# Where GpSimd scales and shifts the residual rows: in the up stages, in half rows through DRAM, not during the down projections

## The chip, the cores and the metric

One core of a Trainium2 chip (trn2) runs the whole program. The metric is the device time of one execution in microseconds (us); three timed executions and one profiled execution of the kernel before are shown.

## The reference

Two layers over 1024 rows of 1024 float32 numbers. Layer 0's mixer is a gated delta network, layer 1's is retention. Cut to what the change touches:

```python
e = silu(c @ cond_w + cond_b)
for i in range(2):
    sh1, sc1, g1, sh2, sc2, g2 = split(e @ ada_w[i] + ada_b[i], 6)
    y = mixers[i](x * (1 + sc1) + sh1)
    x = layer_norm(ALPHA * x + (1 + g1) * y, ln_g[i, 0], ln_b[i, 0])
    gate, up = split((x * (1 + sc2) + sh2) @ ffn_up[i], 2)      # 1024 -> 2 x 2816
    y = (silu(causal_dwconv(gate, ffn_conv_w[i]) + ffn_conv_b[i]) * up) @ ffn_down[i]
    x = layer_norm(ALPHA * x + (1 + g2) * y, ln_g[i, 1], ln_b[i, 1])
```

`layer_norm` standardizes a row, multiplies it by `ln_g` and adds `ln_b`. The kernel keeps the first norm's rows standardized only and folds `ln_g` and `ln_b` into the scale and shift of the feed-forward input. The residual term `ALPHA * x` of the second norm needs the rows with gain and shift applied, and that is the step that the change moves.

## The kernel before

`layer_tail(i, ...)` runs from a layer's mixer output to its end. It has three parts.

**The prologue and the up stage** are `strassen`. Its prologue multiplies the first items by plain blocks and meanwhile builds the combined right-hand blocks T1 to T4 (`build_T` with its closure `rest`, lines 395 to 437: VectorE subtractions and additions of SBUF tiles). Then come pairs of items, `fp` from 0 to 10: a gate item with `conv` behind it (line 1535: the causal convolution on VectorE) and an up item (line 1549: the product with the gate). When the fourth quarter of an up item is done, GpSimd forms the four sums S1 to S4 of the left-hand blocks (line 1556), and the SP queue stores them to the DRAM tile `ad` (line 1540). Weights come in through tiles `wr` (lines 102, 1210 and 1211), which the SP queue loads.

**The down projection** is `proj_gen`: seven products p of 11 steps j. Each step splits a left block (`ar` to `ab`) and a right block (`Bw`, `Br` to `bb`) into two parts: ScalarE rounds the tile, and VectorE subtracts (line 90). TensorE multiplies them on lines 278 to 280.

**The residual rows** of the first norm lie standardized in `x_mid` (DRAM, `xs[0]` and `xs[2]`), and `proj_gen` applies gain and shift on GpSimd. In the first products `gain_half` takes the second 512 rows in eight half rows of 128x512: a load into a `lane` tile by SP (line 1339), a multiplication and an addition (line 1341), and a store to `xg[i + 1]` by GpSimd's own DMA queue (line 1342). In product 2 `xload` loads the first 512 rows from `x_mid` as four whole rows and scales them in place, 16 operations on half rows (line 1349). Later `xload(1, t)` reads the second half back from `xg` without further work, and `finish` (lines 1354 to 1357) adds the residual.

**What sets the order.** No order is written out for most of the program. When it is built, a scheduler places each instruction on its engine's queue as soon as its operands and its buffers are free by the scheduler's own estimate of times; the place in the program text decides among those that are ready. A tag such as `auh` or `lane` is a set of buffers that are handed out in program order: 8 of 128x512 for `auh`, 4 of 128x1024 for `lane`. `after("w")` ties a DMA behind the last weight load of the program text. Each queue then runs strictly in order, and a DMA that waits for a semaphore holds what stands behind it on its queue.

Of the `auh` buffers a layer holds two with the row `rows[i, 2]` (gate of the mixer's output, read on lines 333 or 1354 to the end of the mixer projection), two with `rows[i, 5]`, and four with gain and shift (`gain_rows`, line 198). `trig` (line 1603) takes four for the cosines and sines of layer 1's retention; it stands behind the whole of layer 0 in the program.

`bg_gain` (lines 370 to 387) does the same scaling for the norm between the layers, on 16 half rows: load by SP (line 380), two GpSimd operations (381, 382), store by SP (383). It is not changed.

Of the kernel before, what the change touches and what calls it, by code (L numbers as in the profile page):

```python
# [33 lines left out]
def trunk_kernel(ctx: ExitStack, tc, A):  # L34
# [47 lines left out]
    def hs(half):  # L82
        return slice(half * HALF, (half + 1) * HALF)
# [281 lines left out]
    def gain_rows(n, key, tag="auh"):  # L365
        return [row_load(A[nm][n:n + 1, :], key, sp, tag) for nm in ("ln_g", "ln_b")]
# [895 lines left out]
            return raw  # L1262
        return ablk

    def proj_gen(nj, ablk, wsrc, slots, xsrc, G, final, ln_next, tag, ltags, dst, key, mm=pe.matmul, gate=None, gain=None):
        bal = {nm: BAL[ltags[4] + nm] for nm in ABLK + ("w11", "w21", "w22", "wT1", "wT2", "wT3", "wT4", "n", "h")}
        pa = [tl("aux", [P, 2, HALF], name="pa") for _ in range(4)]
        p1 = [pa[t // 2][:, t % 2] for t in range(4)]
# [61 lines left out]

        xts = [[], []]
        stats = [[], []]
        grows = gain_rows(gain[0], key) if gain else None

        def gain_half(n):
            hf, rs = n // 4, slice(HALF + n % 4 * P, HALF + (n % 4 + 1) * P)
            x = tl("lane", [P, HALF], name="xg")
            with after("w"):
                sp.dma_start(x, gain[1][rs, hs(hf)])
            for r, op in zip(grows, (ALU.mult, ALU.add)):  # L1340
                pool.tensor_tensor(x, x, r[hf], op)
            pool.dma_start(xsrc[rs, hs(hf)], x)

        def xload(half, t):
            xt = load_row(xsrc if half or not gain else gain[1], half, t)
            if half == 0 and gain:
                for r, op in zip(grows, (ALU.mult, ALU.add)):
                    for hf in range(2):
                        pool.tensor_tensor(xt[:, hs(hf)], xt[:, hs(hf)], r[hf], op)
            xts[half].append(xt)  # L1350
            stats[half].append(tl("st", [P, 2, 6]))

        def finish(half, t, nh, c):
# [74 lines left out]
        for p, (an, bn, fin) in enumerate(prods):  # L1428
            accs = acc4() if gate and p < 2 else [acc_next() for _ in range(4)]
            tail = []  # L1430
            depth = ltags[3] if p == 6 else 2
            for j in range(nj):
                if gate and p < 2:
                    yield gate(j)
                    yield from take("qkv", 2)
                    give("qkv", 2)
                a, w = ops(an, bn, j, not gate and p < (7 if final else 5))
                with after("a"):
                    for st in steps[p * nj + j + ahead:p * nj + j + ahead + 1]:
                        load_b(*st)  # L1440
                if gain and p < 2 and j % 2 == 0 and p * 4 + j // 2 < 8 and j < 8:
                    gain_half(p * 4 + j // 2)
                if gain and p == 2 and j % 2 == 0 and j < 8:
                    xload(0, j // 2)
                if p == 2 and j < 4 and gate:
                    xload(0, j)
                    finish(0, j, 0, c11[j])
                if j >= nj - depth:
                    tail.append((j, a, w))
                else:  # L1450
                    for t in range(4):
                        mma(accs[t], t, a, w, j == 0, False, mm if p < 2 else pe.matmul)
                        yield 0.0
                if p == 5 and j > 1:
                    for _ in range(-(-16 // (nj - 2))):
                        if hooks:
                            hooks.pop(0)()
                bg_step()
            if p == 5:
                while hooks:  # L1460
                    hooks.pop(0)()
            if p == 6:
                pin[0] = None
            for t in range(4):
                for j, a, w in tail:
                    mma(accs[t], t, a, w, j == 0, j == nj - 1, mm if p < 2 else pm if p == 6 else pe.matmul)
                fin(t, accs[t])
                yield 0.0
            if p == 1:
                yield "P2"  # L1470
            if p == 4:
                hooks = [] if final else ln_hooks(0, xts[0], tag, ln_next, outs, dst, key, bal["h"])
                hooks += [lambda t=t: xload(1, t) for t in range(4)]
# [12 lines left out]
    def layer_tail(i, mix, wout, xsrc, x_mid, x_out, ln_next, final):  # L1486
        sc2, sh2 = fold(i, 1, 2 * i)
        if i == 0:
            hT0 = []
            get = out_hl(mix)  # L1490
            G1 = rows[0, 2]
            xts = proj_ln(0, GH, get, wout, xsrc, G1, ("x", i))
            hooks = ln_hooks(0, xts, "hTa", lambda: (sc2, sh2), hT0, x_mid, ("mid", i), BAL["gh"])
            xts = proj_ln(1, GH, get, wout, xsrc, G1, ("x", i), hooks=hooks)
            hooks = ln_hooks(1, xts, "hTa", lambda: (sc2, sh2), [], x_mid, ("mid", i))
            for h in hooks[KT:]:
                h()
        else:
            mix.append((sc2, sh2))
            hT0, xts = proj_st(mix[0])  # L1500
        bg_ada(i, 5, "row")
        if i == 0:
            for j in (1, 0, 4, 3):
                bg_ada(1, j, "col")
        cw = vcol(f"ffn_conv{i}")
        cb = vcol(f"ffn_convb{i}")
        ad = dr.tile([NF // 2, 7, P, HALF], F32, tag=f"ad{i}", name=f"ad{i}")
        up = A["ffn_up"][i]

        def pair_items(fp):  # L1510
            g, o = [], []

            def gate_start():
                g.extend(tl("lane", [P, D], name="g") for _ in range(2))

                def gate(q, a, b):
                    dst = g[q // 2][:, hs(q % 2)]
                    if b is None:
                        act.activation(dst, a, AF.Copy)
                    else:  # L1520
                        dve.tensor_tensor(dst, a, b, ALU.add)
                return gate

            def conv():
                for q in range(4):
                    f, hf = 2 * fp + q // 2, q % 2
                    gv = g[q // 2]
                    w = cw[:, 3 * f:3 * f + 3]
                    t = tl("qkv", [P, HALF], name="o")
                    act.activation(t, gv[:, hs(hf)], AF.Copy, scale=w[:, 2:3])  # L1530
                    for j in (1, 2):
                        c0 = HALF if hf else j
                        c1 = HALF * (hf + 1)
                        tv = t[:, c0 - HALF * hf:]
                        dve.scalar_tensor_tensor(tv, gv[:, c0 - j:c1 - j], w[:, 2 - j:3 - j], tv, ALU.mult, ALU.add)  # L1535
                    act.activation(t, t, AF.Silu, bias=cb[:, f:f + 1])
                    o.append(t)

            def store(nm, q):
                sp.dma_start(ad[fp, ABLK.index(nm)], o[q])  # L1540

            def up_start():
                seen = []

                def gated(q, a, b):
                    c = a
                    if b is not None:
                        dve.tensor_tensor(c, a, b, ALU.add)
                    dve.tensor_tensor(o[q], o[q], c, ALU.mult)  # L1549
                    if q != 1:  # L1550
                        store({0: "11", 2: "12", 3: "22"}[q], q)
                    seen.append(q)
                    if len(seen) == 4:
                        for d, x, y, op, nm in ((1, 1, 3, ALU.add, "S1"), (0, 1, 0, ALU.subtract, "S2"),
                                                (2, 2, 0, ALU.subtract, "S4"), (3, 3, 0, ALU.subtract, "S3")):
                            pool.tensor_tensor(o[d], o[x], o[y], op)  # L1556
                            store(nm, d)
                return gated

            return [(up[4 * fp], up[4 * fp + 2], gate_start, conv), (up[4 * fp + 1], up[4 * fp + 3], up_start, None)]  # L1560

        strassen(hT0, xts, sc2, sh2, [it for fp in range(NF // 2) for it in pair_items(fp)])
        slots = {"c": "hTa", "x": "qkv"}
        gb2 = gain_rows(3, ("mid", i), "hTb") if final else None
        return proj_st(proj_gen(NF // 2, ablk_of(ad, "qkv"), A["ffn_down"][i], slots, xg[i + 1], rows[i, 5],
                       (gb2, x_out) if final else None, ln_next, "hTb", ("hTb", "hTa", 8, 6, "f") if final else ("qkv", "hTa", 8, 4, "0"), x_out, ("out", i), gain=(2 * i, x_mid)))

    g1 = two("auh", F32, "g1")
    for nh in range(2):
# [352 lines left out]
```

## Time and profile before

| what | value |
|---|---|
| median of 3 runs | 3033.51 us (3031.15 to 3038.18) |
| the profiled execution | 3032.61 us |
| its span, first to last instruction | 3030.8 us |
| mean granted TensorE clock | 0.971 |
| TensorE busy | 2840.2 us (94%) |
| VectorE busy | 2271.4 us (75%) |
| ScalarE busy | 1316.8 us (43%) |
| GpSimd busy | 672.8 us (22%) |

In the rows PE is TensorE, PEld its weight loads, DVE VectorE, ACT ScalarE, POOL GpSimd and SP the queue that issues most DMAs; a q behind an engine's name is its sequencer. L90 is line 90. Rows of the timeline give the start in us, the duration in us, the engine, line, operation, output and input, and the count of merged instructions. Rows of the stretches give for each engine the busy us and, in brackets, the count of instructions; then the granted clock, the DMA share and GB/s. By the trace, the prologue of layer 0 lies at about 770 to 860 us, its up stage reaches to about 1215, and its down projection to about 1440; in layer 1 the three begin at about 2343, 2440 and 2790.

### The profile page before, as it was taken

What the parts mean: (1) busy time and instruction counts of PE and PEld (TensorE: products, weight loads), DVE (VectorE), ACT (ScalarE), POOL (GpSimd) and SP (SyncE); (2) the same over time, 40 slices, a digit from 0 to 9 for tenths busy, and PEclk for the clock granted to TensorE, in tenths of its full rate; (3) what the DMA queues carried; (4) which work ended last, traced back from release to release, by engine and by line L of the source; (5) the groups of instructions that cost most, each with busy time, mean ns of one, the idle gap of its engine ahead of it and who ended that gap; (6) DMA issues with size and microseconds to landing.
All of it is one profiled execution on the core that took longest, in us unless ns stands there. A gap on an engine that the chain in (4) does not pass through costs nothing. (4 is left out here: it accounts for less than half of the span.)

```text
span 3030.8 us, 38796 instructions
## 1 busy us (share of the span) xinstructions
PE 2840.2 (94%) x13590; PEld 2312.4 (76%) x13590; DVE 2271.4 (75%) x3841; ACT 1316.8 (43%) x2408; POOL 672.8 (22%) x629
## 2 busy tenths in 40 slices
PE   8889998999999999998999999999999899999997
PEld 7768876887778788786777787767777678888785
DVE  5785786545888888998788645566688887778988
ACT  4655555434544445445432442222243544445442
POOL 0410311033021111730023303422200011113704
PEclk9999998999999999999999999999998999999998
DMA  7222221354344545854322444666663332336663
GB/s 271 89 70 74 98 82 62 116 170 138 106 153 151 158 158 182 309 193 141 126 105 98 166 160 144 200 184 186 202 217 132 98 136 104 105 105 227 232 188 108
DMA packets 243027, 450.22 MB, mean 149 GB/s; under 512 B 22928, under 2 KB 76432, under 8 KB 242832
## 3 DMA queue, kind: packets, MB, share of 16 engines
q1 hardware_dynamic: 211648, 400.02, 40.0%
q10 hardware_dynamic: 29760, 43.00, 3.9%
q0 software_dynamic: 1424, 4.72, 0.4%
q8 instruction: 107, 1.75, 0.2%
q14 instruction: 88, 0.72, 0.1%
HBM read 339.13 MB, written 108.53 MB: 148 GB/s over the span
## 5 line engine op out<-in xcount | busy, mean ns | idle before, releaser
L636 PE MATMUL acc<-hT,wh 128*128 128x512 f32 x960 | 302.8, 397 | 0.0
L1556 POOL TENSOR_TENSOR o<-o 128x512 f32<-128x512 f32 x88 | 121.1, 1386 | 725.4 <-DVE o L1549 622.9
L279 PE MATMUL acc<-bb,ab 128*128 128x512 f32 x504 | 205.5, 408 | 18.8 <-DVE bb L90 18.7
L1158 PE MATMUL acc<-T,wb 128*128 128x512 f32 x840 | 205.3, 393 | 8.7 <-DVE wb L90 8.6
L636 PEld LDWEIGHTS acc<-hT,wh 128*128 128x128 f32 x960 | 184.3, 192 | 34.5
L278 PE MATMUL acc<-bb,ab 128*128 128x512 f32 x504 | 192.2, 407 | 16.9 <-DVE ab L90 10.3
L636 PE MATMUL acc<-hT,wl 128*128 128x512 f32 x480 | 204.3, 426 | 0.3 <-ACT sg L1084 0.3
L89 ACT ACTIVATE ab<-ar 128x512 fp32r<-128x512 f32 x210 | 129.8, 624 | 168.6 <-PE acc L280 87.9
L280 PE MATMUL acc<-bb,ab 128*128 128x512 f32 x504 | 202.6, 403 | 0.0
L1158 PEld LDWEIGHTS acc<-T,wb 128*128 128x128 f32 x840 | 157.9, 189 | 46.1 <-DVE wb L90 12.4
L90 DVE TENSOR_TENSOR wb<-wr,wb 128x512 fp32r<-128x512 f32 x162 | 116.0, 718 | 92.8 <-ACT wb L89 89.5
L90 DVE TENSOR_TENSOR ab<-ar,ab 128x512 fp32r<-128x512 f32 x210 | 169.2, 812 | 15.1 <-ACT ab L89 14.7
L90 DVE TENSOR_TENSOR wl<-wr,wh 128x1024 fp32r<-128x1024 f32 x85 | 106.4, 1252 | 89.7 <-ACT wh L89 89.7
L90 DVE TENSOR_TENSOR wb<-mm,wb 128x512 fp32r<-128x512 f32 x216 | 145.1, 683 | 22.8 <-ACT wb L89 20.9
L89 ACT ACTIVATE wh<-wr 128x1024 fp32r<-128x1024 f32 x101 | 106.8, 1058 | 121.3 <-PE acc L636 56.1
L89 ACT ACTIVATE wb<-mm 128x512 fp32r<-128x512 f32 x216 | 122.8, 593 | 72.5 <-DVE mm L1204 72.4
L1215 ACT ACTIVATE pc<-acc 128x512 f32<-128x512 f32 x143 | 84.5, 593 | 154.0 <-PE acc L1158 95.2
L636 PE MATMUL acc<-wh,hT 128*128 128x512 f32 x384 | 138.0, 422 | 2.0 <-DVE vv L90 2.0
L89 ACT ACTIVATE wb<-wr 128x512 fp32r<-128x512 f32 x162 | 99.3, 627 | 92.2 <-DMA wr<-in_ffn_up 45.9
L1535 DVE SCALAR_TENSOR_TENSOR o<-g,vc,o 128x512 f32<-128x512 f32 (+2 forms) x176 | 138.2, 804 | 0.8 <-ACT o L1530 0.2
L457 DVE SCALAR_TENSOR_TENSOR qkv<-raw,vc,qkv 128x512 f32<-128x512 f32 x144 | 114.6, 800 | 30.4 <-ACT qkv L455 29.3
L279 PEld LDWEIGHTS acc<-bb,ab 128*128 128x128 f32 x504 | 98.9, 196 | 44.7 <-DVE bb L90 24.3
(634 smaller groups left out, 7792.0 us busy)
## 6 DMA issues: line engine op xcount, KB each, us to landing
wr<-in_ffn_up SPq DMA_DIRECT2D x96, 512.0 KB, 4.0
mvw<-in_ada_w SPq DMA_DIRECT2D x80, 512.0 KB, 4.3
ad<-o SPq DMA_DIRECT2D x154, 256.0 KB, 2.2
ar<-ad SPq DMA_DIRECT2D x154, 256.0 KB, 4.4
Br<-in_ffn_down SPq DMA_DIRECT2D x88, 256.0 KB, 4.1
wr<-in_ret_wv SPq DMA_DIRECT2D x32, 512.0 KB, 3.7
ar<-od SPq DMA_DIRECT2D x56, 256.0 KB, 5.3
xs<-xt ACTq DMA_DIRECT2D x24, 512.0 KB, 3.8
```

Source lines behind the costliest of these rows:

```text
L89: act.activation(dst_h, src, AF.Copy)
L90: eng.tensor_tensor(dst_l, src, dst_h, ALU.subtract)
L278: mm(acc, a[1][:, sl], w[0], start=first, stop=False)
L279: mm(acc, a[0][:, sl], w[1], start=False, stop=False)
L280: mm(acc, a[0][:, sl], w[0], start=False, stop=last)
L457: dve.scalar_tensor_tensor(oh, raw[:, 3 - j:515 - j], w[:, 3 - j:4 - j], oh, ALU.mult, ALU.add)
L636: pq(pe.matmul(out, lhsT, rhs, start=start, stop=stop), cost)
L1158: return pe.matmul(*a, skip_group_check=True, **kw)
L1215: act.activation(t, X, AF.Copy)
L1535: dve.scalar_tensor_tensor(tv, gv[:, c0 - j:c1 - j], w[:, 2 - j:3 - j], tv, ALU.mult, ALU.add)
L1556: pool.tensor_tensor(o[d], o[x], o[y], op)
```

## The change

The four rows of gain and shift are loaded ahead of the up stage. A function `scale_rows` takes one half row of 128x512 at each call: load from `x_mid` by SP into an `auh` tile, multiplication and addition on GpSimd, store to `xg[i + 1]` by SP. It is called behind each `conv` but the first pair's, and ahead of S1 to S4 of each up item; the first 16 of its 21 calls have a half row to do. `proj_gen` loses `gain_half` and the scaling in `xload`; product 2 now loads the first 512 rows from `xg`, as whole rows.

```diff
@@ proj_gen
-        grows = gain_rows(gain[0], key) if gain else None
-
-        def gain_half(n):
-            hf, rs = n // 4, slice(HALF + n % 4 * P, HALF + (n % 4 + 1) * P)
-            x = tl("lane", [P, HALF], name="xg")
-            with after("w"):
-                sp.dma_start(x, gain[1][rs, hs(hf)])
-            for r, op in zip(grows, (ALU.mult, ALU.add)):
-                pool.tensor_tensor(x, x, r[hf], op)
-            pool.dma_start(xsrc[rs, hs(hf)], x)
-
         def xload(half, t):
-            xt = load_row(xsrc if half or not gain else gain[1], half, t)
-            if half == 0 and gain:
-                for r, op in zip(grows, (ALU.mult, ALU.add)):
-                    for hf in range(2):
-                        pool.tensor_tensor(xt[:, hs(hf)], xt[:, hs(hf)], r[hf], op)
-            xts[half].append(xt)
+            xts[half].append(load_row(xsrc, half, t))
...
-                if gain and p < 2 and j % 2 == 0 and p * 4 + j // 2 < 8 and j < 8:
-                    gain_half(p * 4 + j // 2)
-                if gain and p == 2 and j % 2 == 0 and j < 8:
+                if not gate and p == 2 and j % 2 == 0 and j < 8:
                     xload(0, j // 2)
@@ layer_tail
+        grows = gain_rows(2 * i, ("mid", i))
+        scaled = [(hf, r) for hf in range(2) for r in range(8)]
+
+        def scale_rows():
+            if scaled:
+                hf, r = scaled.pop(0)
+                rs = slice(r * P, r * P + P)
+                x = tl("auh", [P, HALF], name="xg")
+                sp.dma_start(x, x_mid[rs, hs(hf)])
+                for w, op in zip(grows, (ALU.mult, ALU.add)):
+                    pool.tensor_tensor(x, x, w[hf], op)
+                sp.dma_start(xg[i + 1][rs, hs(hf)], x)
...
             def conv():
+                if fp:
+                    scale_rows()
                 for q in range(4):
...
                     if len(seen) == 4:
+                        scale_rows()
                         for d, x, y, op, nm in ((1, 1, 3, ALU.add, "S1"), (0, 1, 0, ALU.subtract, "S2"),
```

More of the change, by code (lines that the diff above doesn't have):

```diff
@@ L1263, in ablk_of, with proj_gen @@
         return ablk
-    def proj_gen(nj, ablk, wsrc, slots, xsrc, G, final, ln_next, tag, ltags, dst, key, mm=pe.matmul, gate=None, gain=None):
+    def proj_gen(nj, ablk, wsrc, slots, xsrc, G, final, ln_next, tag, ltags, dst, key, mm=pe.matmul, gate=None):
         bal = {nm: BAL[ltags[4] + nm] for nm in ABLK + ("w11", "w21", "w22", "wT1", "wT2", "wT3", "wT4", "n", "h")}
@@ L1565, in layer_tail @@
         return proj_st(proj_gen(NF // 2, ablk_of(ad, "qkv"), A["ffn_down"][i], slots, xg[i + 1], rows[i, 5],
-                       (gb2, x_out) if final else None, ln_next, "hTb", ("hTb", "hTa", 8, 6, "f") if final else ("qkv", "hTa", 8, 4, "0"), x_out, ("out", i), gain=(2 * i, x_mid)))
+                       (gb2, x_out) if final else None, ln_next, "hTb", ("hTb", "hTa", 8, 6, "f") if final else ("qkv", "hTa", 8, 4, "0"), x_out, ("out", i)))
     g1 = two("auh", F32, "g1")
```

## The prediction

> **What bounds the kernel now.** I read the page's busy times first, then the table of stretches around the edited stages, the waits of TensorE there, and the timelines of VectorE, GpSimd and SP.
>
> ```profile
> PE 2840.2 (94%) x13590; PEld 2312.4 (76%) x13590; DVE 2271.4 (75%) x3841; ACT 1316.8 (43%) x2408; POOL 672.8 (22%) x629
> ...
> 780.00:860.00 80.00, 65.84 (x277) 50.87 (x276) 72.75 (x111) 44.34 (x75) 6.80 (x4) 0.96 0.31 102
> 2355.00:2440.00 85.00, 70.33 (x296) 54.17 (x296) 74.82 (x114) 43.65 (x74) 6.75 (x4) 0.96 0.31 99
> 860.00:1200.00 340.00, 338.10 (x1488) 275.55 (x1487) 279.91 (x443) 157.00 (x313) 46.23 (x36) 1.00 0.47 152
> 2440.00:2770.00 330.00, 330.00 (x1456) 272.95 (x1455) 246.82 (x372) 154.32 (x261) 50.01 (x36) 1.00 0.33 112
> 1216.00:1246.00 30.00, 25.02 (x104) 19.80 (x104) 30.00 (x32) 13.21 (x30) 21.74 (x17) 0.94 0.97 358
> 2790.00:2860.00 70.00, 64.14 (x267) 51.91 (x266) 69.90 (x72) 30.39 (x54) 51.66 (x29) 0.95 0.77 282
> ```
>
> TensorE is the bound of the whole, and what can be won or lost is the time in which it stands. Read the rows as prologue, up stage, start of the down projection, each for both layers. In the up stage of layer 1 TensorE does 1456 matmuls in 330 us without a gap, 0.227 us each. At that rate the 104 matmuls of 1216 to 1246 fill 23.6 of 30 us and the 267 of 2790 to 2860 fill 60.5 of 70 us: the starts of the down projections lose 6.4 and 9.5 us. There VectorE is busy all the time with 32 and 72 operations, and it is whom TensorE waits for:
>
> ```profile
> PE acc L279 <- DVE bb L90: 5.0, 2, 3.6
> ...
> PE acc L278 <- DVE ab L90: 2.9, 1, 2.9
> ...
> PE acc L279 <- DVE bb L90: 3.0, 1, 3.0
> ```
>
> The timelines of VectorE and GpSimd show why VectorE is late:
>
> ```profile
> 2831.16 0.68 DVE L1305 TENSOR_TENSOR Bw<-Bw 128x512 f32<-128x512 f32 x1
> ...
> 2839.79 1.78 DVE L90 TENSOR_TENSOR ab<-ar,ab 128x512 fp32r<-128x512 f32 x1
> 2841.50 10.99 DVE L1305 TENSOR_TENSOR Bw<-Bw 128x512 f32<-128x512 f32 x1
> ...
> 2841.93 10.01 POOL L1349 TENSOR_TENSOR xt<-xt,rowb 128x512 f32<-128x512 f32 x8
> ...
> 1245.33 17.57 POOL L1341 TENSOR_TENSOR xg<-xg,rowb 128x512 f32<-128x512 f32 x2 [6.47 <-DMA xg<-xs]
> ```
>
> An operation on two SBUF tiles that takes 0.68 us alone takes 1.78 us when it alternates with the scaling, and 10.99 us behind eight scalings in a row. It also goes the other way: two scalings took 17.57 us while VectorE ran without a gap. The two exclude each other. The Trainium skill ("SBUF — State Buffer", section "Who interferes with whom") states that a VectorE instruction with two SBUF inputs and a GpSimd instruction that reads SBUF lock each other out for one instruction; the 10.99 us across eight show a longer hold than that.
>
> **What is removed: 13.3 us won.** The scaling leaves the down projections.
>
> ```profile
> L1556 POOL TENSOR_TENSOR o<-o 128x512 f32<-128x512 f32 x88 | 121.1, 1386 | 725.4 <-DVE o L1549 622.9
> ...
> L1341 POOL TENSOR_TENSOR xg<-xg,rowb 128x512 f32<-128x512 f32 x32 | 81.0, 2536 | 67.0 <-DMA ar<-ad 29.0 <-PE sc L1158 19.4 <-DMA xg<-xs 17.7
> ...
> L1349 POOL TENSOR_TENSOR xt<-xt,rowb 128x512 f32<-128x512 f32 x32 | 55.8, 1777 | 15.9 <-DMA xt<-xs 15.8
> ```
>
> 64 operations and 137 us of GpSimd go from there. The last pair's four sums stay: 4 x 1.386 = 5.5 us of the 21.74 and 51.66 us that GpSimd has in the two stretches, a quarter and a ninth. I let them keep that share of the loss: 6.4 x 0.75 + 9.5 x 0.89 = 13.3 us won. Bounds: 15.9 us if the sums hurt nobody alone, 0 if the switch of stages is what hurts. I stay near the upper one, since VectorE's stretch (30.0 - 32 x 0.655 = 9 us and 69.9 - 72 x 0.655 = 23 us, with 72.75 / 111 = 0.655 us from the prologue's row) exceeds the loss in both. Beyond 2860 nothing is won: the later stops of TensorE have no scaling beside them.
>
> **Where the moved step lands: not where it is written.** `scale_rows` is written between the pairs, but nothing ties its load there, and this kernel's queues run ahead of the text:
>
> ```profile
> 662.62 0.90 SPq L198 DMA_DIRECT2D rowb<-in_ln_g  x2
> ...
> 737.52 0.67 DVE L333 TENSOR_TENSOR t<-acc,g 128x512 f32<-128x512 f32 x1
> ...
> 738.23 0.33 SPq L1603 DMA_DIRECT2D cosT<-in_cosT  x1
> ...
> 759.52 0.67 DVE L333 TENSOR_TENSOR t<-acc,g 128x512 f32<-128x512 f32 x1
> ...
> 760.22 0.33 SPq L1603 DMA_DIRECT2D cosT<-in_cosT  x1
> ```
>
> The gain row that the down projection needs at 1215 is loaded at 662. Each half of the mixer's gate row gives back its `auh` buffer with its last reader on line 333, and within 0.1 us of the reader's end the buffer is taken by a cosine half of the next layer. In the changed kernel the half rows stand ahead of those in the text, so they take the two buffers at 738 and 760. What a unit then costs is told by `bg_gain`, the same step with the same queues:
>
> ```profile
> L380 SPq DMA_DIRECT2D xg<-xs x16: 319/326/742, 1666.9 to 1939.3; - x16
> ...
> DMA to landing us min/median/max: 2.4/3.6/7.5
> ...
> L381 POOL TENSOR_TENSOR xg<-xg,gb x16: 1270/1298/2283, 1682.1 to 1941.9; 128x512 f32<-128x512 f32 x16
> ...
> DMA to landing us min/median/max: 2.0/3.4/6.9
> ```
>
> Load 3.6, two operations of 1.3, store 3.4 (the last row, of line 383): about 10 us, so one unit in 5 us from two buffers. Six units are through by 780; the other ten, 20 operations, run from 780 to about 830. In layer 1 the gate row is read for the last time at these points, and the rows come from the stores of line 363:
>
> ```profile
> 2311.12 0.69 DVE L1354 TENSOR_TENSOR acc<-acc,rowb 128x512 f32<-128x512 f32 x1
> ...
> 2337.55 0.69 DVE L1354 TENSOR_TENSOR acc<-acc,rowb 128x512 f32<-128x512 f32 x1
> ...
> L363 ACTq DMA_DIRECT2D xs<-xt x24: 326/326/444, 712.5 to 2343.4; - x24
> ```
>
> That puts about ten units there too behind 2355. So the step falls into the prologues, not into the up stages.
>
> **What it costs there: 17.3 us.** In the prologues VectorE is busy for 72.75 of 80 and 74.82 of 85 us, mostly with two SBUF inputs, and TensorE already waits for it. An added operation costs VectorE between 0.09 us (the up stage of layer 1: (246.82 - 372 x 0.655) / 36) and 1.10 us (1.78 - 0.68). I take 0.65, nearer to the upper row, since the prologue's operations are of the down projection's kind: 20 x 0.65 = 13 us per layer. VectorE's idle time, 7.25 and 10.2 us, is the cover; I count half of it (3.6 and 5.1), since the rest waits for weights or ScalarE: 9.4 + 7.9 = 17.3 us. With no cover it is 26 us, at the lower price nothing.
>
> **SP: 3 us.** The stores move from GpSimd's queue to SP's, in the order of the text 32 loads and 32 stores instead of 16 loads, and each store waits on SP for GpSimd.
>
> ```profile
> SPq L1540 <- POOL o L1556: 65.0, 79, 3.4
> ...
> SPq L383 <- POOL xg L382: 38.6, 14, 7.1
> ```
>
> 38.6 / 14 = 2.8 us per store, in which a weight load of line 102 or 1210 can stand behind it, and VectorE and TensorE behind that load. Two caught per layer for all of it is 11 us, none is 0; I take 3, since most weight loads wait for their buffers anyway. The bytes themselves are covered by a DMA share of 0.31. Later, the plain row loads in product 2 replace loads of the same size: nothing.
>
> **Sum.** -13.3 + 17.3 + 3 = +7.0 us on the profiled execution's 3032.6 us, 3039.6. The median of the runs is 0.9 us above it, so 3040.5 us. The three runs spread by 0.2%, 6 us, about what a measurement here can tell from no change.
>
> **Rivals.**
>
> *GpSimd waits instead of VectorE* (faster). If VectorE keeps its hold as in the 17.57 us row, the scaling gets in only at gaps that VectorE has anyway, and costs 2 us per layer: -13.3 + 4 = -9.3, 3024 us. For it: in the prologues VectorE runs dense. Against it: once in, the two alternated at 1.78. It decides as soon as an added operation costs under 0.4 us.
>
> *The units stay where they are written* (faster). Then all 32 of a layer lie in the up stage. Layer 1 has 83 us of idle VectorE and no waiting TensorE: 0. Layer 0 has 60 us idle; of 32 x 0.65 = 21 us I let a quarter through: 5 us. Sum -8.3, 3025 us. Against it: the loads at 662, 738 and 760.
>
> *Each operation holds VectorE for its whole length* (slower). At 1.30 us instead of 0.65 the prologues cost 26 - 3.6 and 26 - 5.1 us, 43.3 in place of 17.3: +33, 3066 us. For it: the 10.99 us row, 1.37 us for each of the eight. Against it: 1.10 us in the alternating rows, and VectorE operations in the prologue that read PSUM. The Trainium skill's rule of the lock, taken at its word, is this case.
>
> *SP is held* (slower). GpSimd, kept out by VectorE, keeps SP, and SP the weights. Two holds per layer of 7.1 us in place of the 3: +29.4, 3063 us. It decides when a hold meets an empty `wr` tile.
>
> *The gain stays out* (slower). The sums, the last convolutions and the first splits of the down projection meet in any case; then only the cost remains, +20.3, 3054 us. Against it: the 10.99 us row has no sum beside it, only scalings.
>
> **How the numbers follow.** Forecast 0.40, GpSimd waits 0.22, as written 0.09, whole length 0.04, SP held 0.12, gain stays out 0.13. Within 6 us of the median is 3027.5 to 3039.5. The forecast alone runs from 3033 to 3048 by its price per operation (0.5 to 0.85): 0.02 of its 0.40 goes to faster, 0.11 to same, 0.27 to slower. The faster rivals give 0.26 to faster and 0.05 to same; the slower ones 0.27 to slower and 0.02 to same. Faster 0.28, same 0.18, slower 0.54. The range reaches from 3021, a little under the faster rivals, to 3063, the middle of the held SP: 0.07 lies below, 0.10 above.
>
> **What would show it.** Right: the loads of the half rows begin near 720 to 760 and 2310 to 2340 and are done by 870 and 2440; VectorE operations of 1.78 us and fewer matmuls in the prologues; between 1216 and 1246 and between 2790 and 2860 (shifted) near to full counts of matmuls. Wrong: loads spread over the up stages; prologues as long as before; the start of a down projection losing 5 us or more with no scaling beside it; SP waiting for GpSimd over 7 us while a split waits for `wr`.

## The result and the profile after

The changed kernel takes 3075.1 us, the median of 6 runs, and the kernel before beside it 3035.85, also of 6: a ratio of 1.0131 with an interval of 1.0107 to 1.0156. The forecast was 3040.5 with a range up to 3063: the sign is right, the size is not, and the time lies above the range. The profiled execution took 3076.35 us, with a span of 3074.6, 43.8 more than before's 3030.8.

The page's first part, and the tile `xg` in the changed kernel with its loads, operations and stores (shortest, median and longest in ns, then first and last start):

```profile
PE 2846.7 (93%) x13590; PEld 2319.4 (75%) x13590; DVE 2259.8 (74%) x3841; ACT 1316.6 (43%) x2408; POOL 641.9 (21%) x613
...
L1502 POOL TENSOR_TENSOR xg<-xg,rowb x64: 1262/1705/2269, 724.2 to 2417.5; 128x512 f32<-128x512 f32 x64
L1500 SPq DMA_DIRECT2D xg<-xs x32: 319/320/1239, 718.7 to 2409.5; - x32
L1503 SPq DMA_DIRECT2D xg<-xg x32: 319/320/424, 727.2 to 2419.1; - x32
```

Read the places first. The loads begin at 719 and the last store of layer 1 is issued at 2419, before its up stage begins: the step runs in the prologues. The median of a scaling has gone from the 1.3 us that it takes alone to 1.7. The whole busy time of VectorE and GpSimd did not rise at all; the loss can't be seen in the shares. It is seen in the counts of the stretches. They are the same six as before; the last four are moved by 31 and 54 us, by which the two layers are late at that point:

```profile
780.00:860.00 80.00, 54.49 (x229) 43.13 (x228) 72.70 (x74) 34.03 (x58) 39.93 (x24) 0.85 0.49 159
2355.00:2440.00 85.00, 65.94 (x267) 52.31 (x266) 72.03 (x81) 28.39 (x44) 41.91 (x28) 0.88 0.46 161
891.00:1231.00 340.00, 337.02 (x1481) 274.43 (x1480) 278.95 (x442) 155.43 (x311) 46.23 (x36) 1.00 0.46 152
2494.00:2824.00 330.00, 330.00 (x1454) 272.83 (x1453) 247.04 (x373) 153.21 (x261) 49.40 (x36) 1.00 0.34 114
1247.00:1277.00 30.00, 30.00 (x135) 24.54 (x133) 30.00 (x49) 17.10 (x37) 10.86 (x3) 1.00 0.92 334
2844.00:2914.00 70.00, 70.00 (x310) 58.02 (x309) 48.70 (x74) 33.84 (x60) 6.06 (x2) 1.00 0.68 244
```

In the prologues VectorE is busy for as long as before, 72.70 and 72.03 us, but gets through 74 operations in place of 111 and 81 in place of 114. At 0.655 us each the missing 37 and 33 are 24 and 22 us of VectorE's work. The up stages are as before. The starts of the down projections have full counts: 135 matmuls in 30 us and 310 in 70, where there had been 104 and 267. The 74 more are 16.8 us won.

The timelines of GpSimd and VectorE inside layer 0's prologue show one operation against another:

```profile
783.37 6.60 POOL L1502 TENSOR_TENSOR xg<-xg,rowb 128x512 f32<-128x512 f32 x4 [8.06 <-DMA xg<-xs]
792.50 6.93 POOL L1502 TENSOR_TENSOR xg<-xg,rowb 128x512 f32<-128x512 f32 x4 [2.52 <-DMA xg<-xs]
801.20 26.88 POOL L1502 TENSOR_TENSOR xg<-xg,rowb 128x512 f32<-128x512 f32 x16 [1.78 <-DMA xg<-xs]
...
801.10 0.68 DVE L426 TENSOR_TENSOR bt<-bt 128x512 f32<-128x512 f32 x1
801.70 1.75 DVE L90 TENSOR_TENSOR 12_7077<-bt,12_7077 128x512 fp32r<-128x512 f32 x1
803.38 1.77 DVE L432 TENSOR_TENSOR bt<-bt,hT 128x512 f32<-128x512 f32 x1
805.07 1.74 DVE L90 TENSOR_TENSOR 22_7080<-bt,22_7080 128x512 fp32r<-128x512 f32 x1
```

From 801.7 on, with 16 scalings in a row on GpSimd, VectorE's operations take 1.74 to 1.77 us, where they take 0.68 just before. The two engines take turns, one operation each in about 1.68 us. TensorE's waits from 740 to 900 us name VectorE at the top:

```profile
PE acc L110 <- DVE wl L90: 14.4, 2, 11.7
PE acc L303 <- DVE t L333: 6.8, 1, 6.8
PE acc L111 <- DVE 12_7097 L90: 6.6, 1, 6.6
```

To put the loss into stages I counted matmuls from the table of stretches of 5 us, and took for each kernel the time at which it has done a given number. This is worked out from the single profiled executions, in us later than before. A matmul on the border of two stretches counts in both, so the count runs to about 14600 and not to 13590; it serves only to compare the kernels at the same point of their work:

```
matmuls done           before   changed  no step  tied
 4400 mixer 0, late     721.0     +2.2    +6.4    +1.7
 4600 mixer 0, end      767.2     +7.4    +6.3    +3.4
 4800 prologue 0        812.3    +31.0    +8.1    +7.1
 6600 up stage 0       1205.8    +32.7    +9.4   +16.0
 6800 down 0, start    1254.4    +25.6    +2.8    +9.1
11400 mixer 1, late    2295.7    +27.5    -0.5    +1.8
11600 mixer 1, end     2342.7    +32.5    -0.6    +3.1
11800 prologue 1       2388.1    +54.5    +1.2    +6.7
13400 up stage 1       2738.5    +54.6    +0.6    +8.3
end (span)             3030.8    +43.8   -13.9    -7.1
```

The changed kernel is later by 23.6 and 22.0 us after the two prologues and by about 5 after the tail of each mixer, and wins 7.1 and 10.8 at the down projections.

### The profile page after: what moved, and what is told of

Same layout as the page of the kernel before. It is cut to its first block, busy times and chain, and to the rows that moved or that the text cites. A ratio compares the mean times of both kernels' runs of the same rounds, so it can differ in the third digit from the quotient of the medians.

```text
span 3074.6 us, 38797 instructions
## 1 busy us (share of the span) xinstructions
PE 2846.7 (93%) x13590; PEld 2319.4 (75%) x13590; DVE 2259.8 (74%) x3841; ACT 1316.6 (43%) x2408; POOL 641.9 (21%) x613
## 4 chain that ended last, share of the span: by engine, by line
PE 59%; DVE 20%; issue 8%; DMA 7%; ACT 3%; POOL 2%; SPq 0%; POOLq 0%; DVEq 0%; ACTq 0%
PE acc L636 13%; PE acc L1158 7%; PE acc L110 4%; PE acc L111 4%; PE acc L112 4%; PE sc L1158 3%; PE sc L636 3%; PE acc L278 3%; PE acc L279 3%; PE acc L280 3%; PE mm L636 2%; PE sc L111 1%; PE sc L110 1%; PE sc L112 1%; DVE qkv L457 1%
## 5 line engine op out<-in xcount | busy, mean ns | idle before, releaser
L1554 POOL TENSOR_TENSOR o<-o 128x512 f32<-128x512 f32 x88 | 133.5, 1528 | 757.1 <-DVE o L1546 644.2
L278 PE MATMUL acc<-bb,ab 128*128 128x512 f32 x504 | 191.7, 404 | 17.3 <-DVE xt L1340 8.7
L90 DVE TENSOR_TENSOR ab<-ar,ab 128x512 fp32r<-128x512 f32 x210 | 150.5, 721 | 54.0 <-ACT ab L89 53.6
L90 DVE TENSOR_TENSOR wl<-wr,wh 128x1024 fp32r<-128x1024 f32 x85 | 112.2, 1320 | 85.1 <-ACT wh L89 85.1
L457 DVE SCALAR_TENSOR_TENSOR qkv<-raw,vc,qkv 128x512 f32<-128x512 f32 x144 | 114.8, 801 | 26.4 <-ACT qkv L455 25.1
```

The lines of the kernel that those rows point to most:

```text
L90: eng.tensor_tensor(dst_l, src, dst_h, ALU.subtract)
L278: mm(acc, a[1][:, sl], w[0], start=first, stop=False)
L457: dve.scalar_tensor_tensor(oh, raw[:, 3 - j:515 - j], w[:, 3 - j:4 - j], oh, ALU.mult, ALU.add)
```

## The experiments

My theory A: the GpSimd operations cost, each because it shuts VectorE out while it reads SBUF, and TensorE pays since VectorE has no lead in the prologues. Rival B: the 64 loads and stores on SP, which hold up weight loads. Rival C: the down projections' gain, or the cost, has nothing to do with the place. Except where said otherwise the diffs are against the changed kernel.

**No operations.**

```diff
-                for w, op in zip(grows, (ALU.mult, ALU.add)):
-                    pool.tensor_tensor(x, x, w[hf], op)
```

> The changed kernel without the two GpSimd operations of each half row: the loads and stores stay, gain and shift are left out of the residual rows. Theory A (the two engines exclude each other: 24 added operations in each prologue take VectorE 1.1 us apiece, some 46 us in both layers): the prologues fall back to their old length and the time is 3020 to 3032 us. Rival B (the half rows' DMAs hold SP and the weights come late): the prologues stay long and the time is 3055 to 3075 us.

Measured: 3020.0 us (before beside it 3034.81), ratio 0.9941, interval 0.992 to 0.9962. All of the loss is gone when the 64 operations are gone, though the 64 DMAs are still there. 3075.1 - 3020.0 = 55.1 us, 0.86 us per operation. The prologues' rows, again in the same stretches, have VectorE's counts of before (111 and 114):

```profile
780.00:860.00 80.00, 64.98 (x268) 49.56 (x268) 73.10 (x112) 44.38 (x75) 6.81 (x4) 0.94 0.55 188
2355.00:2440.00 85.00, 71.30 (x282) 55.36 (x281) 74.82 (x115) 41.12 (x70) 7.55 (x5) 0.92 0.33 112
```

**No step at all**: no scaling, no loads, no stores; the down projection reads its rows from `x_mid`.

```diff
-        scaled = [(hf, r) for hf in range(2) for r in range(8)]
+        scaled = []
...
-        return proj_st(proj_gen(NF // 2, ablk_of(ad, "qkv"), A["ffn_down"][i], slots, xg[i + 1], rows[i, 5],
+        return proj_st(proj_gen(NF // 2, ablk_of(ad, "qkv"), A["ffn_down"][i], slots, x_mid, rows[i, 5],
```

> The changed kernel without the step altogether: no half row is loaded, scaled or stored, the residual rows are read standardized only, gain and shift are left out. It measures the term that is won in the down projections. By the record's term it is 13 us faster than the kernel before (3022 us); by the two traces side by side, 18 to 20 us (3016 us). If the switch of stages is what hurts there, it is as slow as before (3035 us).

Measured: 3019.53 us, ratio 0.9945, 0.9931 to 0.996. The gain by itself is 3034.81 - 3019.53 = 15.3 us (12.1 to 20.9 by the interval), and 3019.53 is what a placement that costs nothing would reach. The 32 loads and 32 stores without operations stand 0.5 us above it; the intervals of the two kernels reach 4 to 6 us to either side, so a few us are not ruled out.

**Tied.** Each load is held behind the last weight load that stands ahead of it in the text, so the units run where they are written.

```diff
-        anchor["w"] = sp.dma_start(wr, src)
+        anchor["w"] = anchor["u"] = sp.dma_start(wr, src)
...
-            sp.dma_start(wb, ub)
+            anchor["u"] = sp.dma_start(wb, ub)
...
-                sp.dma_start(x, x_mid[rs, hs(hf)])
+                with after("u"):
+                    sp.dma_start(x, x_mid[rs, hs(hf)])
```

> The changed kernel, with each half row's load tied behind the last weight load that stands ahead of it in the text, so that the units lie in the up stages where they are written; all work is done. Theory A (it is the place, a prologue in which VectorE is the bound, that costs): the prologues have their old length, the gain in the down projections stays, the up stage of layer 0 pays 0 to 8 us: 3016 to 3027 us. Rival C (the operations cost VectorE and so TensorE the same wherever they lie): 3060 to 3080 us.

Measured: 3028.29 us, ratio 0.9983, 0.9965 to 1.0; 46.8 us less than the changed kernel with the same 64 operations and 64 DMAs. That settles rival C: the same work costs by its place. The tile's row and the two up stages:

```profile
L1503 POOL TENSOR_TENSOR xg<-xg,rowb x64: 1277/1452/9852, 787.5 to 2672.8; 128x512 f32<-128x512 f32 x64
...
860.00:1200.00 340.00, 333.37 (x1458) 269.97 (x1457) 282.42 (x432) 153.00 (x308) 82.49 (x62) 1.00 0.54 176
2440.00:2770.00 330.00, 330.00 (x1453) 272.43 (x1452) 255.15 (x372) 151.00 (x257) 86.65 (x62) 1.00 0.38 130
```

The time is a little over the 3027 that I gave as the top. In layer 0's up stage, where VectorE is busy for 280 of 340 us, TensorE does 1458 matmuls instead of 1488: 30 x 0.227 = 6.8 us. In layer 1's, where VectorE has 83 us idle, 1453 instead of 1456.

Idle time of VectorE is not all that differs there. A unit comes alone, with two scalings, and many of VectorE's operations in the up stage read the matmul's result `acc` from PSUM, so that only one of their inputs lies in SBUF. Two units of layer 0, each as GpSimd's row and VectorE's row beside it:

```profile
887.09 3.44 POOL L1503 TENSOR_TENSOR xg<-xg,rowb 128x512 f32<-128x512 f32 x2 [10.78 <-DMA xg<-xs]
888.19 2.89 DVE L1533 SCALAR_TENSOR_TENSOR o<-g,vc,o 128x512 f32<-128x512 f32 x2
...
908.88 2.66 POOL L1503 TENSOR_TENSOR xg<-xg,rowb 128x512 f32<-128x512 f32 x2 [18.36 <-DMA xg<-xs]
910.15 1.30 DVE L1546 TENSOR_TENSOR acc<-acc,pc 128x512 f32<-128x512 f32 x2 [1.32 <-ACT pc L1215]
```

Two convolution operations, which read two SBUF tiles, take 2.89 us beside the scalings and 1.41 at 896. Two operations on `acc` take 1.30 us beside the scalings, 0.65 each, and the two scalings 2.66, 1.33 each: neither is held. How much of the up stage's low price comes from this and how much from VectorE's idle time is not separated here.

The interval ends at 1.0: the tied kernel may be up to 0.35% faster than before, and is not shown to be. It is the lowest median of all the kernels here that do the whole computation.

**Stores on GpSimd's queue.**

```diff
-                sp.dma_start(xg[i + 1][rs, hs(hf)], x)
+                pool.dma_start(xg[i + 1][rs, hs(hf)], x)
```

> The changed kernel with the half rows' stores on GpSimd's DMA queue, so that SP no longer waits for GpSimd. Theory A: only what is lost ahead of the prologues, at the end of the mixers' projections, can come back, at most 14 us: 3061 to 3076 us. Rival B (held SP): 3030 to 3045 us.

Measured: 3070.88 us, ratio 1.0113, 1.0084 to 1.0143. Rival B falls as the main cause: taking these stores' waits on GpSimd away from SP brings 4 us, and the two intervals overlap.

**One operation instead of two.**

```diff
-                for w, op in zip(grows, (ALU.mult, ALU.add)):
+                for w, op in zip(grows, (ALU.mult,)):
```

> The changed kernel with only the multiplication on GpSimd; the addition of the second gain row is left out, loads and stores stay. Theory A (each GpSimd operation in the prologues takes about 1.1 us from VectorE and so from TensorE; 24 behind 780 and as many in layer 1, the rest in the mixers' tails): the cost over the kernel without operations (3020.0) is 55.1 us for 64 operations; half of them cost half, 3048 (3041 to 3055). Theory C (what costs is the chain of load, operation and store, of which there are still 32): 3065 or more. Theory D (one operation per load fits into the gaps of VectorE, only several in a row lock it out): under 3032.

Measured: 3046.85 us, ratio 1.0045, 1.0027 to 1.0062. 26.9 us over no operations, for 32 of them: 0.84 us each, as with 64. The cost goes with the number of operations, and no gap of VectorE swallows the first ones.

**Fills instead of scalings.**

```diff
-                for w, op in zip(grows, (ALU.mult, ALU.add)):
-                    pool.tensor_tensor(x, x, w[hf], op)
+                for n in range(2):
+                    pool.memset(x, 1.0)
```

> The changed kernel with two GpSimd fills of the same tile by a constant in the place of the multiplication and the addition; so the scaling is left out, GpSimd still writes the same tiles, at the same places, between the same loads and stores, but reads no SBUF. Theory A (VectorE and GpSimd exclude each other because both read two SBUF tiles): 3018 to 3030, near the kernel without operations, and VectorE's operations of 1.78 us are gone from 787 to 828. Theory B (GpSimd being busy, or writing SBUF, is enough): 3060 to 3080 if a fill is as long as a scaling; if it is shorter, the cost shrinks with its length only.

Measured: 3026.28 us, ratio 0.9963, 0.9949 to 0.9977. The tile's row, and GpSimd and VectorE at the place where the changed kernel had its 16 scalings:

```profile
L1502 POOL MEMSET xg<- x64: 524/527/533, 722.7 to 2374.2; 128x512 f32 x64
...
800.21 5.09 POOL L1502 MEMSET xg<- 128x512 f32 x10 [4.59 <-DMA xg<-xs]
...
800.88 0.68 DVE L436 TENSOR_TENSOR bt<-hT,bt 128x512 f32<-128x512 f32 x1
801.48 0.69 DVE L426 TENSOR_TENSOR bt<-bt 128x512 f32<-128x512 f32 x1
802.08 0.69 DVE L437 TENSOR_TENSOR bt<-bt,hT 128x512 f32<-128x512 f32 x1
```

A fill is 0.53 us long, 0.41 of a scaling's 1.29. If the length alone counted, 64 fills would cost 0.41 x 55.1 = 22.6 us; this kernel stands 6.3 us above the one without operations (0.10 each), the two intervals overlap, and by the counts its prologues are 1.7 us longer and 0.3 shorter than before's. VectorE's operations on two SBUF tiles stay at 0.68 to 0.69 us beside ten fills in a row. So it is reading that shuts VectorE out, not that GpSimd is busy or that it writes. This agrees with the Trainium skill ("SBUF — State Buffer", section "Who interferes with whom"), which puts the exclusion down to ports that the two engines share: a VectorE instruction with two SBUF inputs contends with a GpSimd instruction that reads SBUF, not with one that only writes it.

**Tied in layer 1 alone**, layer 0 as before (a short form of the diff, against the kernel before; the loads are tied as above):

```diff
+        scaled = [(hf, r) for hf in range(2) for r in range(8)] if i else []
...
-                       (gb2, x_out) if final else None, ln_next, "hTb", ("hTb", "hTa", 8, 6, "f") if final else ("qkv", "hTa", 8, 4, "0"), x_out, ("out", i), gain=(2 * i, x_mid)))
+                       (gb2, x_out) if final else None, ln_next, "hTb", ("hTb", "hTa", 8, 6, "f") if final else ("qkv", "hTa", 8, 4, "0"), x_out, ("out", i), gain=None if i else (0, x_mid)))
```

> Layer 0 as in the kernel before (scaling in the down projection); layer 1 changed, with each load of a half row tied behind the last weight load ahead of it in the text, so that its units spread over the up stage. Theory A (the stages add up, each for itself): by the running count of matmuls the tied kernel went from +1.8 us at 11400 matmuls to -10 at the end against before, so 11.8 us are won in layer 1 and nothing is lost in layer 0: 3023 (3018 to 3028). Theory B (a gain of one layer is given back in the other, or the tied load costs the weights their order): 3029 or more.

Measured: 3032.81 us, ratio 0.9989, 0.9977 to 1.0001. I had given 3023, a miss by 10 us; theory B's 3029 or more holds as a number. Its profile has full stretches where layer 1's down projection starts:

```profile
2800.00:2840.00 40.00, 40.00 (x178) 33.14 (x177) 33.76 (x53) 19.19 (x34) 7.36 (x2) 1.00 0.94 351
2840.00:2880.00 40.00, 40.00 (x179) 33.10 (x178) 19.89 (x32) 18.79 (x34) 0.00 (x0) 1.00 0.39 114
```

So the gain is there as well; but its execution was 8.1 us behind before at 4000 matmuls (638 us), ahead of every edit. What I had added up from single executions doesn't carry so far. The sum was also wrong in itself: by the spans the tied kernel goes from +1.8 to -7.1 us, 8.9 won in layer 1, not 11.8.

**Tied, without the first pair** (against the tied kernel). A third unit stands in the pairs with `fp` 6 and 7, so the sixteenth comes in pair 7 and not in pair 8:

```diff
+                if fp > 5:
+                    scale_rows()
...
-                        scale_rows()
                         for d, x, y, op, nm in ((1, 1, 3, ALU.add, "S1"), (0, 1, 0, ALU.subtract, "S2"),
...
                             store(nm, d)
+                        if fp:
+                            scale_rows()
```

> The tied kernel with the units of the first pair left out (two more in each of the last two pairs) and the unit beside the four sums put behind them, so that no sum waits for it. Theory A (a unit costs only where it meets a prologue; the tied kernel still loses about 6 us in layer 1 to the units at 2365 to 2415 and some in layer 0 at 787 to 812): 3022 (3018 to 3027). Theory B (what is left of the tied kernel's cost lies in layer 0's up stage, 9 us spread evenly over it, where VectorE is busy for 280 of 340 us): 3026 to 3031, no better than the tied kernel by more than 3 us.

Measured: 3035.07 us, ratio 1.0009, 0.9999 to 1.002: neither A's 3022 nor B's 3026 to 3031. One place alone costs 8 us in its profile, at 1100. The rows of SP, of VectorE and of TensorE there, and the stretch:

```profile
1086.48 5.98 SPq L1605 DMA_DIRECT2D sinT<-in_sinT  x2
1093.83 0.33 SPq L1504 DMA_DIRECT2D xg<-xg  x1
1094.21 0.42 SPq L377 DMA_DIRECT2D gb<-in_ln_g  x1
1095.88 0.33 SPq L377 DMA_DIRECT2D gb<-in_ln_b  x1
1096.26 1.45 SPq L210 DMA_DIRECT2D mvw<-in_ada_w  x3
1107.99 0.34 SPq L1210 DMA_DIRECT2D wr<-in_ffn_up  x1
...
SPq L1605 <- POOL xg L1503: 5.1, 1, 5.1
...
1102.16 0.75 DVE L216 SCALAR_TENSOR_TENSOR ada<-mvw,e,ada 128x512 f32<-128x512 f32 x1 [3.27 <-DMA mvw<-in_ada_w]
...
PE sc L1158 <- DVE wb L90: 4.3, 1, 4.3
...
1100.00:1110.00 10.00, 5.71 (x15) 4.22 (x14) 7.83 (x13) 2.93 (x5) 0.00 (x0) 0.66 0.48 169
```

With the last half rows of the layer done, their two `auh` tiles go to loads for the next layer. One of them (`sinT`) keeps SP for 5.1 us until GpSimd is done with its tile, so the background loads `mvw` behind it are issued at 1096.26 (in the tied kernel at 1089.91). VectorE stands 3.3 us for their data, the split of the next weight block comes behind that and two convolution operations, and TensorE waits for it for 4.3 us. It does 15 matmuls in 10 us there instead of 45, at a granted clock of 0.66. The next weight load, at 1107.99, waited for VectorE to free its buffer and is late as a consequence. I had not seen that the units' tiles keep those loads back while they last.

**Half 1 later** (against the kernel before): half 1's rows are scaled in the products 3 and 4 of the down projection.

```diff
-            x = tl("lane", [P, HALF], name="xg")
+            x = tl("auh", [P, HALF], name="xg")
...
-                if gain and p < 2 and j % 2 == 0 and p * 4 + j // 2 < 8 and j < 8:
-                    gain_half(p * 4 + j // 2)
+                if gain and 2 < p < 5 and j % 2 == 0 and j < 8:
+                    gain_half((p - 3) * 4 + j // 2)
```

> The kernel before with one thing moved: the scaling of half 1's rows stands in the down projection's products 3 and 4 instead of 0 and 1, into auh tiles. There the kernel before has an idle GpSimd and VectorE busy for 29.7 of 40 us (2880 to 2920). Theory A (a scaling costs only where VectorE has no idle time beside it): the start of the down projections is rid of half of its scalings, about 5 us of the 10 in layer 1 and 5 of the 6.5 in layer 0 come back and little is paid: 3025 (3021 to 3029). Theory B (16 operations cost 1.1 us each wherever VectorE works, or the scalings of half 0, which stay, hold the start up by themselves): 3032 or more.

Measured: 3044.33 us (before beside it 3036.98), ratio 1.0021, 1.0006 to 1.0035: slower, and theory B's 3032 or more holds as a number. Its profiled execution is only 1.0 us over the first one of before, so that execution shows where time is won and lost, but not the loss of the median. The move had a side effect that I had not meant: half 1 no longer holds `lane` tiles, which half 0's rows take too, and half 0's 16 scalings in layer 0 now begin at 1255 instead of 1284. First GpSimd and a stretch of this kernel, then the same of the kernel before:

```profile
1254.93 26.82 POOL L1349 TENSOR_TENSOR xt<-xt,rowb 128x512 f32<-128x512 f32 x16 [7.74 <-DMA xt<-xs]
...
1260.00:1270.00 10.00, 7.17 (x31) 5.43 (x30) 10.00 (x7) 3.46 (x6) 10.00 (x7) 1.00 0.99 370
```

```profile
1284.36 28.52 POOL L1349 TENSOR_TENSOR xt<-xt,rowb 128x512 f32<-128x512 f32 x16 [9.23 <-DMA xt<-xs]
...
1290.00:1300.00 10.00, 10.00 (x46) 8.29 (x45) 10.00 (x7) 4.62 (x8) 10.00 (x7) 1.00 0.48 159
```

These two stretches are the clearest lesson of the study. In both, VectorE is busy for all of 10 us with 7 operations, and GpSimd with 7. The collision is the same; TensorE does 46 matmuls in one and 31 in the other, and by the count of matmuls this kernel loses 13.4 us in this place. From 1250 to 1320 TensorE waits for nobody in the kernel before, and in this one for VectorE:

```profile
PE sc L278 <- DVE ab L90: 9.1, 3, 4.4
```

My reading was that VectorE had split ahead when the scalings came in the one, and had no lead in the other. The lead can be counted from the two timelines: steps with both blocks split, less the matmuls on these blocks at 12 to a step. In the kernel before it is 4.8 steps at 1285, where its scalings begin, and never under 3 until they end. In this kernel it is 5.5 steps at 1245, 1.8 at 1255, where its scalings begin, and 0 at 1275. What took it before they began shows in the rows of GpSimd and VectorE:

```profile
1234.16 13.03 POOL L1556 TENSOR_TENSOR o<-o 128x512 f32<-128x512 f32 x2 [6.93 <-DMA ad<-o]
...
1251.32 0.69 DVE L1305 TENSOR_TENSOR Bw<-Bw 128x512 f32<-128x512 f32 x1 [6.54 <-DMA Bw<-in_ffn_down]
```

Two of the last pair's four sums, shut out by a dense VectorE, took 13.03 us. SP waited 10.6 us to store one of them and issued no load of `Bw` from 1235 to 1247, so VectorE then stood 6.54 us for `Bw`.

**Split**: half 1 as in the last kernel, half 0 in the up stages from the second pair on, each load tied (against it; a short form, with the tie as above):

```diff
+        scaled = [(hf, r) for hf in range(2) for r in range(4)]
...
+                        if fp:
+                            scale_rows()
+                        if fp == 3:
+                            scale_rows()
```

> Half 1's rows as in the kernel with the later half; half 0's rows scaled in the up stages, one half row per pair from the second pair on (two in the fourth), each load tied behind the last weight load ahead of it in the text. So no scaling is left in a prologue or at the start of a down projection. Theory A (place decides, and 8 units in 300 us of an up stage are cheap): near the kernel without the step (3019.5), 3022 (3018 to 3027), better than the tied kernel (3028.3) and than before. Theory B (a scaling costs 1.1 us of TensorE's time or a late weight load in the up stage and the later products too; 64 x 0.3 us in the tied kernel): 3028 or more.

Measured: 3043.55 us, ratio 1.0023, 1.0009 to 1.0037. Slower, so A's 3022 is a plain miss and B's 3028 or more holds as a number. To see whether single profiles can carry such sums I ran before and this kernel once more, unchanged.

> The kernel before, unchanged, for a second profile. In the stretch up to 4000 matmuls (638 us), where all the kernels here have the same order of work, the profiles so far stand between 5.7 us ahead of the first profile of before and 10.7 us behind it. Theory P (that offset belongs to a kernel as it is laid down): this one is within 2 us of the first profile there. Theory X (it belongs to the single execution): anywhere between -6 and +11, most likely more than 2 us away.

> The split kernel, unchanged, a second time. Its first profile was 10.7 us behind before at 4000 matmuls, ahead of all that was edited, and 11.9 us behind at the end. Theory P (the offset belongs to a kernel): again 8 to 12 us behind at 4000 matmuls and a median of 3040 to 3047. Theory X (it belongs to the execution): within -6 to +6 us there, and a median of 3031 to 3037, so that the small differences between the placements told apart by their medians are not to be trusted under some 10 us.

Measured: before 3032.67 us, and 1.1 us behind its first profile at 4000 matmuls; the split kernel 3046.73 us, ratio 1.0045, 1.0028 to 1.0061, with an offset of 0.0 us there where its first profile had 10.7. The second profile of before agrees with P, that of the split kernel only with X: one kernel's offset can move by 10.7 us from execution to execution. Yet the median came out above before again, as P had it: the split kernel is slower, by 0.2 to 0.5%. Part of where, its second profile shows; the up stages of the two layers, 16 operations in each:

```profile
860.00:1200.00 340.00, 332.63 (x1455) 268.93 (x1454) 281.31 (x433) 152.74 (x308) 68.18 (x50) 1.00 0.49 162
2440.00:2770.00 330.00, 329.06 (x1444) 270.43 (x1443) 251.25 (x370) 149.42 (x255) 70.91 (x50) 1.00 0.36 123
```

Layer 0's lacks 33 matmuls against before, 7.5 us, or 0.47 per operation if it is all theirs; layer 1's lacks 12, 2.7 us. So VectorE's idle 60 us in layer 0 did not hide the 16 operations. What is left of this kernel's loss I have not taken apart.

## Why the prediction was wrong

**What held.** The place: loads from 719 and 2318 on, the last scalings over at 828 and 2419 inside the prologues, the down projections freed. The direction followed from it. The upper bound, 1.10 us per operation from the rows of 1.78 and 0.68, was near the truth as well; I did not take it.

**The step that failed: the price in the prologues.** The sum had 17.3 us; the count of matmuls gives 23.6 + 22.0 = 45.6. Three choices made it.

- *0.65 us per operation, between 0.09 and 1.10.* I went down from the upper row without a row for it. The lower end came from the up stage of layer 1, where VectorE has time to spare; it could not be a bound for stretches without any. In the prologue VectorE's operations took 1.74 to 1.77 us, the upper row itself; the kernels without and with the two operations differ by 0.86 us of the whole time for each, the ones in the mixers' tails included.
- *20 operations.* 24 came behind 780 and, by the timeline, as many behind 2355 in layer 1. The rows of `x_mid` had a part in that: SP waited for their stores, which I had left out in layer 0 when I let a unit run every 5 us from the first free tile. From 715 to 860, the times SP waited:

```profile
SPq L1503 <- POOL xg L1502: 23.3, 12, 5.1
SPq L1500 <- DMA xs<-xt: 19.3, 4, 8.6
```

- *Half of VectorE's idle time as cover, 3.6 and 5.1 us.* It covered nothing: VectorE was busy for 72.70 us of 80 after, as before. Its idle time in layer 0's prologue is mostly a wait for ScalarE's rounding of the weights, 8.9 us before and 8.4 after: it was still there when VectorE was late.

With 24 operations at 1.10 us and no cover it would have been 26.4 us per layer, a little over the 23.6 and 22.0 found.

**Left out: the mixers' tails.** 8 operations ran there in each layer, and the count is 5.2 and 5.0 us later behind them. The sum had nothing for that. In layer 1 it goes with the operations: the kernel without them loses 0.5 us there. In layer 0 it does not: the kernel without operations loses 4.3 us there and the one with fills 4.0, the kernel without the step nothing. There the untied loads and stores on SP are what is left; by which wait they cost this is open.

**The gain: 13.3 us said, 15.3 measured** by the kernel without the step (16.8 by the counts of the two starts). The 13.3 lies inside that interval too. The four sums that I let keep a quarter and a ninth of the loss hurt nobody in the changed kernel: two of them were held for 12.93 us at 1269, and TensorE's count there is full. With scalings behind them they can hurt, as the kernel with the later half shows.

**SP: 3 us said, 0.5 measured, and not told apart.** By the medians the DMAs alone cost 0.5 us, with the few us of doubt given above. Without the stores' waits on GpSimd (in layer 1's prologue up to 8.1 us, 42.8 in all) the changed kernel was 4 us faster, inside its interval.

Against the profiled execution the sum is 7.0 and the count 43.8: prologues +28.3, tails +10.2, gain -4.6, SP -3, and 5.9 us in the stretches between, which is within the scatter of one execution against another. The 3 us of SP are taken as not found here, though the tails hold some of it.

**The rivals.** The one that each operation holds VectorE for its whole length, 3066 us, was nearest, at 0.04; its mechanism is nearly right (1.10 of 1.30 us) and its count was short by the tails and by eight operations. "GpSimd waits" is not what happens in the changed kernel: with 16 scalings ready in a row the two engines alternate. (Where a single unit comes it can be so: the tied kernel's longest scaling is 9.85 us.) "SP is held" was added up wrongly: 4 x 7.1 us in place of the 3 gives +32.4, 3066 us and not 3063, and 3075 lies above that as well. The run with the stores on GpSimd's queue leaves it about 4 us of the median in the changed kernel; in the kernel with the later half it is seen once, with 10.6 us. The two faster rivals left the 3 us of SP out of their sums. "As written" is what the tied kernel makes true; there the forecast of 3025 is 3 us off. "The gain stays out" is ruled out by the kernels without operations and without the step, both 15 us under before.

## What to carry to other kernels

Where one engine's operation and another's exclude each other, price each by the alternating rows of the trace in full. Take a lower value only for a stretch in which a row shows that the two do not meet: operations that read one input from PSUM, or an engine that has nothing to do. Whether TensorE then pays is another question: count the lead of the shut-out engine there, and don't go by its share of busy time. And a step whose load is tied to nothing runs where its tile comes free, not where it is written; if the place matters, tie it.

## What the runs showed beyond that

The exclusion is of reads: a GpSimd fill of the same tile cost 0.10 us by the medians, a scaling 0.86, and in the rows of the tied kernel beside VectorE operations that read PSUM neither engine was held. The same 7 operations against 7 in 10 us cost TensorE nothing with a lead of 4.8 steps and 15 matmuls with one of 1.8. And two executions of the split kernel differ by 10.7 us before the first edit is reached, so a sum of stages from a single profile is good to about that, while its medians of 12 and 4 runs agreed within 3.2 us. What makes that offset is open, and so are the loss in layer 0's mixer tail and most of the split kernel's loss.
